# Softmax division moved from the attention weights to the attention output, query scale moved to the layout of the queries, and the SSD half of the output projection traced after attention

## Chip, cores and metric

One core of one Trainium2 chip. The metric is the device time of one execution of the whole kernel in microseconds (us), here the median of 3 runs.

## The reference, cut

Two layers, 512 tokens of 1024 features. Each layer has a mixer and a feed-forward part. The mixer projects its normalised input at once into the queries, keys and values of an attention group and into the inputs of a state-space (SSD) group; the two group outputs stand side by side and go through one output projection.

```python
q = rms_norm(q.reshape(b, l, N_Q_HEADS, HEAD_DIM), q_norm_w[i])   # 8 query heads of 64
k = rms_norm(k.reshape(b, l, N_KV_HEADS, HEAD_DIM), k_norm_w[i])  # 2 key heads
q = axial_rope(q, ...); k = axial_rope(k, ...)
# blocked_gqa, with q / sqrt(64):
s = jnp.einsum("bqgrd,bkgd->bgrqk", qi, k)
p = jax.nn.softmax(s, axis=-1)
attn_out = jnp.einsum("bgrqk,bkgd->bqgrd", p, v)
...
mixed = jnp.concatenate([attn_out, ssd_out], axis=-1)
x = x + jnp.einsum("ble,ed->bld", mixed, w_out[i])
```

## The kernel before, in words

All products run in pairs of reduced-precision operands: a weight or activation is split into a high part and a low part (`whi`/`wlo`, `xh`/`xl`), and `mm3` (lines 409 to 413) adds three matmuls for one product. The weights come in chunks through `Stream`: SP loads a chunk, ACT casts its high part (line 192), DVE or POOL subtracts the low part (line 193). `next` splits two chunks ahead.

The mixer of a layer is written as three generators that `drain` steps in turn: `att` (attention), `fill` (the projections of q, z and the convolution inputs, then the output projection) and `ssd`. The order in which they are stepped is the order of tracing. A scheduler at compile time then fixes the order on each engine: it plays the program on a model of the engines, and whenever an engine is free, it takes the instruction traced earliest among those that are ready; `tc.high_priority()` puts what is traced within it ahead of the rest. On the chip each engine runs its instructions in that fixed order.

Attention works on 8 blocks of a layer, each 128 queries (`c`, 4 of them) by 4 heads of one key head (`g`, 2 of them); the blocks of `g` = 0 come first. For a block, `queries` (line 650) copies the four heads into `qd`, each twice side by side (line 653, ACT), transposes them on PE (line 656) and splits them into `qh` (line 659, ACT) and `ql` (line 660, DVE). `attention` (line 663) then does for each of the 4 heads:

- two matmuls into the scores, 128 queries by 512 keys (lines 668 and 669, PE);
- the negated maximum of a row (line 671, DVE) and its product with the scale `qri` (line 672, DVE), the reciprocal norm of the query;
- the exponential with that scale and bias, and its row sum into `sm` (line 674, ACT);
- the reciprocal of the sum (line 675, DVE) and the division of the weights, 128x512, in place (line 679, DVE);
- four transposes (line 682, PE), their copy into `t_ring` (line 684, ACT, shown as L92), and for two heads together 16 small matmuls with the values (line 692, PE), whose result is copied into `qr` (line 694, ACT, shown as L92).

`qri` is worked out once for each `g` by a row of small DVE instructions (lines 637 and 285 to 291).

The SSD half of the output is the first half of `out_half` (line 787): 8 outputs of 12 matmuls each, added into `part` (line 795, DVE). It needs only the SSD group. It is traced once the SSD generator is done, while attention has some blocks left. After it and after attention, the attention output is cast and subtracted, four times (lines 854 and 855), and the attention half of `out_half` follows (line 933).

Of the kernel before, what the change touches and what calls it, by code (L numbers as in the profile page):

```python
# [15 lines left out]
F32 = mybir.dt.float32  # L16
# [3 lines left out]
ALU = mybir.AluOpType  # L20
# [16 lines left out]
NPAIR = (NF - PLAIN) // 2  # L37
SRAW = 6

NORM = "VVVV"  # L40
PTE = "AAAA"
GGE = "GG"
QDE, OUTE, _, YE, HE, WE, RAE, MLE, DSE = "AAVGVGVVG"
EB, GGB = 2, 4
DDW, DDE = 512, "A"
MORE = "VGGVG"
# [28 lines left out]
def bc(ap, shape, axis):  # L75
    return ap.unsqueeze(axis).broadcast_to(shape)
# [3 lines left out]
def tile_hybrid_encoder(ctx, tc, xt_d, par_d, rope_d, snw_d, w_kvdt, w_xbc, w_q, w_z, w_out, w_gate, w_up, w_down, out_d):  # L80
# [10 lines left out]
    def copy(e, out, in_):  # L91
        A.copy(out, in_) if e == "A" else (G if e == "G" else V).tensor_copy(out, in_)  # L92
# [353 lines left out]
    def mixer(l, norm, mx):  # L446
# [203 lines left out]
        def queries(c, g):  # L650

            qd = mx.tile([P, 4, 2, 64], F32, name="qd", tag="qd")
            copy(QDE, qd, bc(qr[:, c, 4 * g:4 * g + 4], [P, 4, 2, 64], 2))
            tp = bank("t")
            for j in range(4):
                T.transpose(tp[:, j * P:(j + 1) * P], qd[:, j].rearrange("p a d -> p (a d)"), ident)
            qh = mx.tile([P, S], F32R, name="qh", tag="qh", bufs=2)
            ql = mx.tile([P, S], F32R, name="ql", tag="ql", bufs=2)
            A.copy(qh, tp)
            V.tensor_tensor(ql, tp, qh.bitcast(F32), ALU.subtract)  # L660
            return qh, ql

        def attention(c, g, qh, ql):
            nm = mx.tile([P, 4], F32, name="nm", tag="nm", bufs=2)
            sm = mx.tile([P, 4], F32, name="sm", tag="sm", bufs=2)
            for j in range(4):
                s_ = bank("s")
                T.matmul(s_, lhsT=qh[:, j * P:(j + 1) * P], rhs=KK[:, g], start=True, stop=False)
                T.matmul(s_, lhsT=ql[:, j * P:(j + 1) * P], rhs=KK[:, g], start=False, stop=True)
                ri = qri[g][:, c, j:j + 1]  # L670
                V.tensor_reduce(nm[:, j:j + 1], s_, AX.X, ALU.max, negate=True)
                V.tensor_tensor(nm[:, j:j + 1], nm[:, j:j + 1], ri, ALU.mult)
                p_ = ring("p")
                A.activation(p_, s_, AF.Exp, bias=nm[:, j:j + 1], scale=ri, accum_out=sm[:, j:j + 1])
                V.reciprocal(sm[:, j:j + 1], sm[:, j:j + 1])
                if NORM[j] == "A":
                    A.activation(p_, p_, AF.Copy, scale=sm[:, j:j + 1])
                else:
                    (G if NORM[j] == "G" else V).tensor_scalar(p_, p_, sm[:, j:j + 1], None, ALU.mult)
                t_ = bank("t")  # L680
                for kt in range(NC):
                    T.transpose(t_[:, kt * P:(kt + 1) * P], p_[:, kt * P:(kt + 1) * P], ident)
                pt = merge(ring("t"), NC, P)
                copy(PTE[j], pt, merge(t_, NC, P))
                if j % 2 == 0:
                    first = pt
                    continue
                o_ = bank(O_BANK)

                for kt in range(NC):  # L690
                    for e, t2 in enumerate((first, pt)):
                        T.matmul(o_[64 * e:64 * e + 64, :P], lhsT=Vt[:, kt, g * 64:(g + 1) * 64],
                                 rhs=t2[:, kt], start=kt == 0, stop=kt == NC - 1)
                copy(OUTE, qr[:, c, 4 * g + j - 1:4 * g + j + 1].rearrange("p h d -> p (h d)"), o_[:, :P])
                yield
# [91 lines left out]
        def out_half(half, order, src, x, nxt=None):  # L787
            for n, m in enumerate(order):
                if n % 2 == 0:
                    wh, wl = W.next()  # L790
                ps = bank("a")
                for k in range(4):
                    o = (n % 2 * 4 + k) * P
                    mm3(ps, wh[:, o:o + P], wl[:, o:o + P], mixed, half * 4 + k, k == 0, k == 3)
                V.tensor_tensor(x[m], src[m], ps, ALU.add)
                if nxt is not None and m >= 4:
                    nxt.tile(m)
                    nxt.square(m)
                if m % 2:
                    yield  # L800
# [21 lines left out]
        def fill():  # L822
            for what in ORDER:
                i = int(what[1])
                if what[0] == "q":
                    yield from qproj(i)
                elif what[0] == "z":
                    yield from token_major(lambda c: bank("a"), op, 256, z_done(i))
                else:
                    xbc(i)  # L830
                    yield
                    if all(f"x{j}" in ORDER[:ORDER.index(what) + 1] for j in range(4, 8)):
                        done.append("BC")
                    if sum(w_[0] == "x" for w_ in ORDER[:ORDER.index(what) + 1]) == 8:
                        for c in range(3):
                            state(0, c)
                        for c in (3, 2, 1):
                            state(1, c)
                        done.append("conv")
            done.append("z")  # L840
            while "ssd" not in done:
                yield

            part = [mx.tile([P, S], F32, name=f"part{i}", tag=t) for i, t in enumerate(sorted(Htags))]
            part += [mx.tile([P, S], F32, name=f"part{6 + i}", tag="ee", bufs=EB) for i in range(2)]
            for k in range(KT):
                nc.sync.dma_start(part[k], (xt_d if l == 0 else x_save)[k])
            yield from out_half(1, range(KT), part, part)
            while "att" not in done:
                yield  # L850
            for j in range(4):
                src = qr.rearrange("p c (j a) d -> p j c (a d)", a=2)[:, j]
                h = mixed.h[j].rearrange("p (c q) -> p c q", c=NC)
                A.copy(h, src)
                tt(MLE, mixed.l[j].rearrange("p (c q) -> p c q", c=NC), src, h.bitcast(F32), ALU.subtract)
            Z["part"] = part

        def drain(*gens):
# [7 lines left out]
        def att():  # L866
            todo = [(c, g) for g in range(2) for c in range(NC)]
            ready = None
            for i, (c, g) in enumerate(todo):
                while g not in qri:  # L870
                    yield
                now = ready or queries(c, g)
                ready = None
                if i + 1 < len(todo) and todo[i + 1][1] in qri:
                    ready = queries(*todo[i + 1])
                yield from attention(c, g, *now)
            done.append("att")

        def finish(cs):
# [288 lines left out]
```

## Time and profile before

| | us |
|---|---|
| median of 3 runs | 1262.58 (1261.21 to 1265.16) |
| the profiled execution | 1260.2 |
| its span, first to last instruction | 1258.5 |
| mixer of layer 0, about | 0 to 282 |
| mixer of layer 1, about | 630 to 895 |

Engines: PE is TensorE's matmuls, PEld its weight loads, DVE VectorE, ACT ScalarE, POOL GpSimd, SP SyncE. The span is the part of the execution that the trace shows; 1.7 us of the profiled execution lie around it. Busy time of PE counts matmuls whose ends are modelled and overlap, so a PE that is busy throughout is not necessarily at its peak.

### The profile page before, as it was taken

How to read it: one execution, taken by the hardware profiler on the slowest of the kernel's cores; microseconds unless marked ns; L12 is line 12 of the kernel's file. 1: busy time of each engine (PE TensorE's matmuls, PEld its weight loads, DVE VectorE, ACT ScalarE, POOL GpSimd, SP SyncE). 2: the span in 40 equal slices, each digit the busy share in tenths (PEclk: the TensorE clock that was granted, in tenths of full speed). 3: DMA queues.
4: the chain of work that ended last, by engine and by line, in shares of the span. 5: the costliest groups of instructions: out<-in, count | busy, mean ns of one | idle time of the engine just before them, and what ended most of it. 6: DMA issues, size and time to landing. Idle time of an engine off the chain costs nothing.

```text
span 1258.5 us, 19786 instructions
## 1 busy us (share of the span) xinstructions
PE 1205.1 (96%) x7694; PEld 1066.4 (85%) x7694; DVE 962.1 (76%) x1593; ACT 620.1 (49%) x1147; POOL 249.3 (20%) x208
## 2 busy tenths in 40 slices
PE   6898998999999999999998999999999999999996
PEld 6787887687899899899897787777878999999995
DVE  8899789656887577577679989985688856856853
ACT  4566655634354244255455575753453533533544
POOL 6523655010200000000234255520120000000002
PEclk8999998999999999999999999989999999999998
DMA  5321122032434324321442202112243233243122
GB/s 170 104 72 51 34 68 77 17 101 65 154 96 143 89 83 132 88 87 32 135 135 89 67 30 72 55 40 72 94 144 88 98 117 113 74 120 114 34 63 80
DMA packets 47533, 110.04 MB, mean 87 GB/s; under 512 B 5424, under 2 KB 5936, under 8 KB 47440
## 3 DMA queue, kind: packets, MB, share of 16 engines
q1 hardware_dynamic: 47440, 108.79, 27.4%
q8 instruction: 60, 0.98, 0.3%
q14 instruction: 33, 0.27, 0.1%
HBM read 104.44 MB, written 4.33 MB: 86 GB/s over the span
## 4 chain that ended last, share of the span: by engine, by line
PE 76%; DVE 17%; ACT 3%; issue 2%; POOL 1%; DMA 1%; DVEq 0%; ACTq 0%; POOLq 0%
PE ps_a L1030 6%; PE ps_a L1029 5%; PE ps_a L1028 5%; PE ps_a L411 4%; PE ps_a L412 3%; PE ps_a L413 3%; PE ps_a L1075 3%; PE ps_a L1074 3%; PE ps_a L1076 3%; PE ps_s L1074 3%; PE ps_s L1075 3%; PE ps_s L1076 3%; PE ps_s L1030 3%; PE ps_s L1029 3%; PE ps_s L1028 3%; DVE u L594 3%
## 5 line engine op out<-in xcount | busy, mean ns | idle before, releaser
L192 ACT CAST whi<-wraw 128x512 fp32r<-128x512 f32 (+4 forms) x185 | 126.7, 713 | 231.7 <-PE ps_a L412 61.5
L192 ACT CAST whi<-sraw 128x1024 fp32r<-128x1024 f32 x126 | 131.7, 1050 | 141.3 <-DVE sraw L167 40.4
L193 DVE TENSOR_TENSOR wlo<-sraw,whi 128x1024 fp32r<-128x1024 f32 x126 | 153.6, 1223 | 46.5 <-ACT whi L192 46.3
L323 POOL TENSOR_TENSOR ssq<-ssq,sqt 128x512 f32<-128x512 f32 x17 | 25.7, 1511 | 679.5 <-ACT sqt L320 679.3
L193 DVE TENSOR_TENSOR wlo<-wraw,whi 128x512 fp32r<-128x512 f32 (+4 forms) x121 | 109.1, 911 | 49.8 <-ACT whi L192 48.8
L411 PE MATMUL ps_a<-xh,whi 128*128 128x512 f32 x320 | 126.3, 397 | 3.2 <-DVE a__9140 L971 1.6
L413 PE MATMUL ps_a<-xh,wlo 128*128 128x512 f32 x320 | 126.0, 394 | 0.0
L412 PE MATMUL ps_a<-xl,whi 128*128 128x512 f32 x320 | 125.7, 394 | 0.0
L193 POOL TENSOR_TENSOR wlo<-wraw,whi 128x512 fp32r<-128x512 f32 x64 | 91.1, 1441 | 97.8 <-ACT whi L192 90.7
L167 DVE TENSOR_TENSOR sraw<-sraw 128x1024 f32<-128x1024 f32 x72 | 88.0, 1222 | 1.0
L419 PE MATMUL ps_a<-whi,xh 128*128 128x256 f32 (+1 forms) x256 | 75.5, 297 | 7.9 <-ACT whi L192 7.8
L1030 PE MATMUL ps_a<-ss,wlo 128*128 128x256 f32 x288 | 81.7, 284 | 0.0
L1028 PE MATMUL ps_a<-ss,whi 128*128 128x256 f32 x288 | 81.5, 283 | 0.0
L1029 PE MATMUL ps_a<-ss,whi 128*128 128x256 f32 x288 | 81.5, 283 | 0.0
L1030 PE MATMUL ps_a<-s,wlo 128*128 128x256 f32 x288 | 81.1, 283 | 0.0
L1029 PE MATMUL ps_a<-s,whi 128*128 128x256 f32 x288 | 81.1, 283 | 0.0
L1028 PE MATMUL ps_a<-s,whi 128*128 128x256 f32 x288 | 79.8, 283 | 0.0
L420 PE MATMUL ps_a<-wlo,xh 128*128 128x256 f32 (+1 forms) x256 | 75.8, 296 | 1.7 <-DVE wlo L193 1.7
L411 PEld LDWEIGHTS ps_a<-xh,whi 128*128 128x128 f32 x320 | 60.2, 188 | 17.1 <-ACT s L989 4.0
L421 PE MATMUL ps_a<-whi,xl 128*128 128x256 f32 (+1 forms) x256 | 74.4, 293 | 0.0
L413 PEld LDWEIGHTS ps_a<-xh,wlo 128*128 128x128 f32 x320 | 60.4, 189 | 13.2 <-issue 0.8
L412 PEld LDWEIGHTS ps_a<-xl,whi 128*128 128x128 f32 x320 | 60.3, 188 | 12.4 <-DVE xl L809 0.4
(393 smaller groups left out, 3601.8 us busy)
## 6 DMA issues: line engine op xcount, KB each, us to landing
sraw<-in_w_gate SPq DMA_DIRECT2D x72, 256.0 KB, 3.8
sraw<-in_w_up SPq DMA_DIRECT2D x72, 256.0 KB, 3.8
wraw<-in_w_down SPq DMA_DIRECT2D x48, 384.0 KB, 3.1
wraw<-in_w_xbc SPq DMA_DIRECT2D x16, 512.0 KB, 3.3
wraw<-in_w_out SPq DMA_DIRECT2D x16, 512.0 KB, 3.3
wraw<-in_w_q SPq DMA_DIRECT2D x8, 512.0 KB, 3.2
wraw<-in_w_z SPq DMA_DIRECT2D x8, 512.0 KB, 3.6
wraw<-in_w_gate SPq DMA_DIRECT2D x8, 512.0 KB, 3.3
```

The costliest lines, as they stand in the source:

```text
L167: V.tensor_tensor(q[to], q[to], q[by], ALU.add)
L192: A.copy(hi[:, u], raw[:, u])
L193: (G if lo_pool else V).tensor_tensor(lo[:, u], raw[:, u], hi[:, u].bitcast(F32), ALU.subtract)
L411: T.matmul(ps, lhsT=wh, rhs=op.h[k], start=first, stop=False)
L412: T.matmul(ps, lhsT=wh, rhs=op.l[k], start=False, stop=False)
L413: T.matmul(ps, lhsT=wl, rhs=op.h[k], start=False, stop=last)
L420: T.matmul(ps, lhsT=xh, rhs=wl, start=False, stop=False)
L1028: T.matmul(out, lhsT=wh[:, o:o + P], rhs=x_[:, 0, i], start=first and i + j == 0, stop=False, skip_group_check=True)
L1029: T.matmul(out, lhsT=wh[:, o:o + P], rhs=x_[:, 1, i], start=False, stop=False, skip_group_check=True)
L1030: T.matmul(out, lhsT=wl[:, o:o + P], rhs=x_[:, 0, i], start=False, stop=i == 3, skip_group_check=True)
L1074: T.matmul(ps[:, cols], lhsT=w1[:, o:o + P], rhs=h, start=f == a, stop=False)
L1075: T.matmul(ps[:, cols], lhsT=w1[:, o:o + P], rhs=g, start=False, stop=False)
```

## The change

The weights stay undivided. The row sums of all 32 heads and query blocks of a layer are kept in one tile, `sums`, and the output is divided at the end by a new function, `normalize`: reciprocal of all sums, 4 transposes to bring heads onto partitions, a copy, then for each pair of heads one f32 matmul that spreads the 8x512 reciprocals over 128 partitions with a matrix of ones and zeros, a product with the output, and the same cast and subtraction as before. The scale `qri` is applied by the copy into `qd`, which becomes four copies of one head each; the product of line 672 goes. `att` ends with `normalize` under high priority, after the z projection, and the SSD half of the output is traced only after `att` has ended.

```diff
         def queries(c, g):
             qd = mx.tile([P, 4, 2, 64], F32, name="qd", tag="qd")
-            copy(QDE, qd, bc(qr[:, c, 4 * g:4 * g + 4], [P, 4, 2, 64], 2))
+            for j in range(4):
+                A.activation(qd[:, j], bc(qr[:, c, 4 * g + j], [P, 2, 64], 1), AF.Copy, scale=qri[g][:, c, j:j + 1])
...
+        sums = mx.tile([P, NC, 8], F32, name="sums")
+        def normalize():
+            sel = ring("p")[:8]
+            G.memset(sel, 0.0)
+            pick = merge(sel, 8, 64)
+            G.affine_select(out=pick, in_=pick, pattern=[[-1, 8], [0, 64]], compare_op=ALU.not_equal, fill=1.0,
+                            base=0, channel_multiplier=1)
+            rec = mx.tile([P, NC, 8], F32, name="rec")
+            V.reciprocal(rec, sums)
+            tp = bank("t")
+            for c in range(NC):
+                T.transpose(tp[:8, c * P:(c + 1) * P], rec[:, c], ident)
+            rows = ring("p")[:8]
+            A.copy(rows, tp[:8])
+            for j in range(4):
+                b = bank("s")
+                T.matmul(b, lhsT=sel[:, j * P:(j + 1) * P], rhs=rows, start=True, stop=True)
+                o = qr.rearrange("p c (j a) d -> p j c (a d)", a=2)[:, j]
+                V.tensor_tensor(o, o, merge(b, NC, P), ALU.mult)
+                h = merge(mixed.h[j], NC, P)
+                A.copy(h, o)
+                tt(MLE, merge(mixed.l[j], NC, P), o, h.bitcast(F32), ALU.subtract)
...
         def attention(c, g, qh, ql):
-                V.tensor_tensor(nm[:, j:j + 1], nm[:, j:j + 1], ri, ALU.mult)
                 p_ = ring("p")
-                A.activation(p_, s_, AF.Exp, bias=nm[:, j:j + 1], scale=ri, accum_out=sm[:, j:j + 1])
-                V.reciprocal(sm[:, j:j + 1], sm[:, j:j + 1])
-                if NORM[j] == "A":
-                    A.activation(p_, p_, AF.Copy, scale=sm[:, j:j + 1])
-                else:
-                    (G if NORM[j] == "G" else V).tensor_scalar(p_, p_, sm[:, j:j + 1], None, ALU.mult)
+                A.activation(p_, s_, AF.Exp, bias=nm[:, j:j + 1], accum_out=sums[:, c, 4 * g + j:4 * g + j + 1])
...
-            yield from out_half(1, range(KT), part, part)
             while "att" not in done:
                 yield
-            for j in range(4):
-                src = qr.rearrange("p c (j a) d -> p j c (a d)", a=2)[:, j]
-                h = mixed.h[j].rearrange("p (c q) -> p c q", c=NC)
-                A.copy(h, src)
-                tt(MLE, mixed.l[j].rearrange("p (c q) -> p c q", c=NC), src, h.bitcast(F32), ALU.subtract)
+            yield from out_half(1, range(KT), part, part)
...
                 yield from attention(c, g, *now)
+            while "z" not in done:
+                yield
+            with tc.high_priority():
+                normalize()
             done.append("att")
```

## Rows read from the trace of the kernel before

**Rows 1.** The page of the profile: its first part (busy time of each engine, share of the span, instructions) and the head of its fourth part (share of the span that each engine has of the chain of work that ended last).

```profile
PE 1205.1 (96%) x7694; PEld 1066.4 (85%) x7694; DVE 962.1 (76%) x1593; ACT 620.1 (49%) x1147; POOL 249.3 (20%) x208
...
PE 76%; DVE 17%; ACT 3%; issue 2%; POOL 1%; DMA 1%; DVEq 0%; ACTq 0%; POOLq 0%
```

**Rows 2.** Busy time of each engine by stretch. Columns: the stretch, its length, then for PE, PEld, DVE, ACT and POOL the busy us with the instruction count, the granted TensorE clock, the DMA share, GB/s. The first five are stretches of the two mixers in which attention runs, the last two those in which the SSD half of the output projection runs.

```profile
84.00:117.00 33.00, 29.24 (x175) 23.52 (x174) 32.09 (x58) 18.76 (x39) 14.02 (x10) 1.00 0.16 50
200.00:236.50 36.50, 30.28 (x208) 23.13 (x206) 32.13 (x85) 22.64 (x59) 13.67 (x12) 0.91 0.18 58
695.00:725.00 30.00, 29.40 (x166) 23.13 (x165) 28.90 (x57) 16.28 (x34) 9.31 (x7) 1.00 0.21 70
770.00:785.00 15.00, 14.09 (x95) 11.36 (x95) 14.19 (x28) 8.03 (x18) 11.71 (x11) 1.00 0.30 90
800.00:845.00 45.00, 40.12 (x286) 32.33 (x284) 42.66 (x106) 30.12 (x78) 19.54 (x18) 0.92 0.18 58
236.50:258.40 21.90, 21.90 (x106) 17.36 (x106) 10.38 (x17) 6.53 (x13) 0.00 (x0) 1.00 0.15 49
845.00:872.00 27.00, 27.00 (x145) 21.44 (x144) 12.43 (x23) 9.06 (x19) 0.00 (x0) 1.00 0.18 59
```

**Rows 3.** The chain of work that ended last, in order of time (start us, us, what): its pieces of half a microsecond or more on lines 672 and 679 and on the subtraction of line 855 (all subtractions of helper `tt` on DVE show as L95).

```profile
104.56 1.36 DVE p_ring L679
...
165.25 0.64 DVE nm L672
...
188.22 0.71 DVE nm L672
...
189.03 1.16 DVE p_ring L679
...
190.29 1.08 DVE p_ring L679
...
203.43 3.36 DVE xl L95 x2
206.79 1.13 DVE nm L672
...
700.67 1.84 DVE p_ring L679 x2
...
719.56 1.32 DVE p_ring L679
...
775.08 1.14 DVE nm L672
...
779.70 0.50 DVE p_ring L679
...
807.58 1.28 DVE p_ring L679 x2
...
813.08 1.69 DVE xl L95
...
815.92 0.60 DVE xl L95
```

**Rows 4.** Busy time by stretch of the instructions of one line alone, for the first five stretches of Rows 2; the sum over the five, in this order for line 672, line 675 and line 679.

```profile
sum 159.50, DVE 7.62; mean DVE 1.52
...
sum 159.50, DVE 5.03; mean DVE 1.01
...
sum 159.50, DVE 21.07; mean DVE 4.21
```

**Rows 5.** Who PE waited for (us in total, times, longest), 195 to 240 us and 800 to 845 us.

```profile
PE ps_m L775 <- DVE y L770: 4.2, 1, 4.2
...
PE ps_m L775 <- DVE y L770: 3.6, 1, 3.6
```

**Rows 6.** Busy time by stretch, columns as in Rows 2: the stretches right after those two waits.

```profile
209.00:217.00 8.00, 8.00 (x36) 6.15 (x35) 7.31 (x20) 0.27 (x1) 5.13 (x5) 0.57 0.29 99
...
815.00:830.00 15.00, 11.36 (x56) 9.54 (x58) 14.39 (x28) 3.88 (x9) 8.27 (x7) 0.77 0.44 141
```

**Rows 7.** The chain of work again, columns as in Rows 3: the product of a 128x128 f32 operand with 512 f32 columns of line 344, which runs as two instructions, and four transposes of a head.

```profile
40.06 0.86 PE ps_m L344 x2
...
139.28 0.44 PE ps_t L682 x4
```

**Rows 8.** Groups of instructions by line, each form apart: count, then busy us, mean ns, and idle time before with its releaser. The copy of four heads into `qd`, and the copy of 128 columns out of PSUM into `qr`.

```profile
L92 ACT COPY qd<-qr 128x512 f32<-128x512 f32 x16 | 10.1, 631 | 3.6 <-DVE qr L95 3.5
L92 ACT COPY qr<-ps_t 128x128 f32<-128x128 f32 x32 | 8.5, 267 | 13.9 <-PE ps_t L692 13.4
```

**Rows 9.** Instructions of one line (count: ns least/median/most, first and last start): the reciprocal of line 486, 64 columns.

```profile
L486 DVE RECIPROCAL sp<-sp x2: 545/550/554, 40.6 to 653.3; 128x64 f32<-128x64 f32 x2
```

**Rows 10.** Instructions in order of time (start us, us, engine, line, operation): the last cast and subtraction of lines 854 and 855 in layer 0, the first POOL instruction after the SSD group with the idle time before it; in layer 1 the last step of the scale `qri` for the second four heads, and the first copy into `qd` that belongs to them.

```profile
250.33 0.62 ACT L854 CAST xh<-qr 128x512 fp32r<-128x512 f32 x1
250.98 0.69 DVE L95 TENSOR_TENSOR xl<-qr,xh 128x512 fp32r<-128x512 f32 x1
...
268.62 1.86 POOL L323 TENSOR_TENSOR ssq<-ssq,sqt 128x512 f32<-128x512 f32 x1 [45.68 <-ACT sqt L320]
...
762.18 0.49 DVE L291 SCALAR_TENSOR_TENSOR qri<-qri1t,qri 128x16 f32<-128x16 f32 x1
...
777.26 0.62 ACT L92 COPY qd<-qr 128x512 f32<-128x512 f32 x1
```

More of the change, by code (lines that the diff above doesn't have):

```diff
@@ L38 @@
 SRAW = 6
-NORM = "VVVV"
 PTE = "AAAA"
 GGE = "GG"
-QDE, OUTE, _, YE, HE, WE, RAE, MLE, DSE = "AAVGVGVVG"
+OUTE, _, YE, HE, WE, RAE, MLE, DSE = "AVGVGVVG"
 EB, GGB = 2, 4
@@ L661, in queries @@
             return qh, ql
+        sums = mx.tile([P, NC, 8], F32, name="sums")
[20 more added lines that the diff above has]
+                tt(MLE, merge(mixed.l[j], NC, P), o, h.bitcast(F32), ALU.subtract)
         def attention(c, g, qh, ql):
             nm = mx.tile([P, 4], F32, name="nm", tag="nm", bufs=2)
-            sm = mx.tile([P, 4], F32, name="sm", tag="sm", bufs=2)
             for j in range(4):
@@ L669, in attention @@
                 T.matmul(s_, lhsT=ql[:, j * P:(j + 1) * P], rhs=KK[:, g], start=False, stop=True)
-                ri = qri[g][:, c, j:j + 1]
                 V.tensor_reduce(nm[:, j:j + 1], s_, AX.X, ALU.max, negate=True)
-                V.tensor_tensor(nm[:, j:j + 1], nm[:, j:j + 1], ri, ALU.mult)
                 p_ = ring("p")
-                A.activation(p_, s_, AF.Exp, bias=nm[:, j:j + 1], scale=ri, accum_out=sm[:, j:j + 1])
-                V.reciprocal(sm[:, j:j + 1], sm[:, j:j + 1])
-                if NORM[j] == "A":
-                    A.activation(p_, p_, AF.Copy, scale=sm[:, j:j + 1])
-                else:
-                    (G if NORM[j] == "G" else V).tensor_scalar(p_, p_, sm[:, j:j + 1], None, ALU.mult)
+                A.activation(p_, s_, AF.Exp, bias=nm[:, j:j + 1], accum_out=sums[:, c, 4 * g + j:4 * g + j + 1])
                 t_ = bank("t")
```

## The prediction

> **What bounds the kernel now.** Begin with the page: PE is busy 96% of the span and holds 76% of the chain of work that ended last, DVE 17% [rows 1]. Averages hide stages, so the second view is busy time by stretch. In the stretches of the mixers where attention runs, DVE is the full engine: 32.09 of 33.00 us, 28.90 of 30.00, 14.19 of 15.00, and in the two late ones 32.13 of 36.50 and 42.66 of 45.00 [rows 2], in which it also waits for others. Once the SSD half of the output runs, this turns round: PE is busy 21.90 of 21.90 and 27.00 of 27.00 us, DVE under half [rows 2]. So a mixer is a DVE stage followed by a PE stage, and what the change takes from DVE counts only in the first. The third view is the chain itself: it passes through the very instructions that go, in 14 pieces of half a microsecond or more [rows 3]. The fourth is what PE waits for: in either layer its longest wait near the end of attention, 4.2 and 3.6 us, is for an addition (line 770) that stands on DVE behind such instructions [rows 5], and after it the granted clock averages 0.57 and 0.77 [rows 6], between its two levels of 1.2 and 2.4 GHz.
>
> **The change part by part.**
>
> *A, DVE is relieved.* For each of 64 heads the scale product, the reciprocal and the division go. In the five DVE stretches they take 7.62 + 5.03 + 21.07 = 33.7 us [rows 4]; the early subtractions of line 855, for the heads of `g` = 0, move out of this crowd to the end and add 3.36 + 1.69 + 0.60 = 5.65 us [rows 3]. That is 39.4 us, the upper bound: it would all be gained if DVE alone set the pace. The pieces that the chain itself passes through are, layer 0, 1.36 + 0.64 + 0.71 + 1.16 + 1.08 + 3.36 + 1.13 = 9.4 us and, layer 1, 1.84 + 1.32 + 1.14 + 0.50 + 1.28 + 1.69 + 0.60 = 8.4 us [rows 3], 17.8 us together. This is the nearer figure, since a piece beside the chain needs another queue to move too; but in four of the five stretches DVE idles under 6% [rows 2], and there a removed instruction moves everything behind it up. I take a quarter of the way from the one to the other: 17.8 + 0.25 x 21.6 = 23.2 us. The lower bound is 10 us, about half the chain's pieces, if PE or the exponential is late next.
>
> *B, the clock.* A stretch of t us at a granted share s loses t(1 - s): 8.00 x 0.43 = 3.4 and 15.00 x 0.23 = 3.4 us [rows 6]. Both follow the waits for line 770 [rows 5]. In layer 0 the removed pieces just ahead of it (3.36 + 1.13) exceed the wait of 4.2; in layer 1 (1.69 + 0.60) they cover two thirds of 3.6. With shorter waits some of the loss should go; I take half, 3.4 us, of 0 to 6.9.
>
> *C, PE gets new work.* Nothing in the trace has 8 partitions and 512 f32 columns; the nearest is line 344, 0.86 us for 128 partitions and as many columns [rows 7]. Four of them are 3.44 us. Four transposes cost 0.44 [rows 7], here with 8 columns of weights each. That is 3.9 us a layer, 7.8 in all. They fall next to the SSD half, where PE has no idle time [rows 2], so I charge them in full; the other end is 0, if they run while PE still waits for the SSD group.
>
> *D, ACT.* One copy of 0.631 us becomes four, of 128 columns each; the nearest row is the 0.267 us copy out of PSUM [rows 8], so 4 x 0.267 - 0.631 = 0.44 us a block, 7.0 us for 16 blocks. The queries are laid out a block ahead, and ACT is busy 95.8 of the 159.5 us of the five stretches (18.76 + 22.64 + 16.28 + 8.03 + 30.12) [rows 2]. I charge 1 us of 0 to 7. The copy also has a new wait, for `qri`. On ACT the exponentials would queue behind it. But for the second group of layer 1 the scale is ready at 762.7 and the first copy starts at 777.26 [rows 10]: 14 us of cover, charged at nothing. Without it, the layout of a block (some 3 us) would show once for each group and layer.
>
> *E, the end of attention.* All sums must be there before the reciprocal. Then follow, one behind another: reciprocal of 32 columns, at most the 0.55 us of 64 [rows 9], transposes 0.44, a copy 0.62, the first spreading matmul 0.86 [rows 7], product 0.69, cast 0.62, subtraction 0.69 [rows 10], and for the other three pairs 2 x 0.69 each on DVE: 0.55 + 0.44 + 0.62 + 0.86 + 0.69 + 0.62 + 0.69 + 4.14 = 8.6 us. The cover is the SSD half: 21.9 us or more in which PE has other work and DVE is free for 11.5 [rows 2]. It was already what hid the end of attention, whose last cast came at 250.33, inside it [rows 10]. POOL's memset and selection have no later work to delay: POOL then idles until 268.62 [rows 10]. The products and casts need no queue but ACT's and DVE's; SP's loads of weights and of `part` are issued as before, though the split of the last SSD chunks is now traced behind attention. I charge E nothing while the SSD half fills it.
>
> *Sum.* -23.2 - 3.4 + 7.8 + 1.0 = -17.8 us on the profiled execution's 1260.2, so 1242.4. The median of the runs stands 2.4 above that execution; the same offset gives **1245 us**.
>
> **The rivals.**
>
> *PE's idle time is the cap.* In the five stretches PE is busy 29.24 + 30.28 + 29.40 + 14.09 + 40.12 = 143.1 of 159.5 us [rows 2]. If that busy time can't be pressed together, A and B are worth at most 16.4 us, and with C and D the time is 1262.6 - 16.4 + 8.8 = 1255. Against it: PE counts as busy for 8.00 of 8.00 us at a clock share of 0.57 [rows 6], so its busy time holds air. The Trainium skill (Perfetto Trace Analysis, Identifying the Most-Contended Engine) says that matmul busy share is no good measure of PE's headroom and that the share of weight loads should be read. By that rule the room is 159.5 less 113.5 us of PEld [rows 2], 46 us, and the cap would not bind, which leaves my sum as it is. Chance 0.20.
>
> *DVE was the whole bound.* The 39.4 us come in full, the clock stays up (6.9), and half of C falls into PE's idle time: 1262.6 - 39.4 - 6.9 + 3.9 + 1.0 = 1221. For it: DVE's busy share over 94% in four of the five stretches [rows 2]. Against it: the chain passes through less than half of that time [rows 3]. Chance 0.15.
>
> *PE waits out the normalisation.* PE runs in a fixed order. If the order made at compile time puts the spreading matmuls ahead of SSD products that are ready, PE stands through the chain of E less its own 1.3 us, 7.3 us a layer, and such a wait is followed by a low clock, as those of 4.2 and 3.6 us were [rows 5, 6], for 3.4 more, and B does not come. That is 2 x 10.7 = 21.4: 1262.6 - 23.2 + 21.4 + 8.8 = 1270, slower than before. It decides from (23.2 - 8.8) / 2 = 7.2 us of lost PE time a layer on. For it: high priority and tracing ahead of the SSD half invite it, and the model of the engines at compile time need not know the waits of the chip. Against it: the order picks among what is ready, and the SSD half is ready during that time in the trace before. Chance 0.15.
>
> **How the numbers follow.** Forecast 0.50, 1234 to 1256 (A some ten us larger or smaller); the cap 0.20; the whole bound 0.15; the wait 0.15. About 0.3%, 3.8 us, is what a measurement of this kernel can tell from no change, so "the same" is 1258.8 to 1266.4. Faster: 0.48 of the forecast, 0.14 of the cap (it reaches up with the upper ends of C and D), 0.15 of the whole bound: 0.77. Slower: 0.12 of the wait. The rest, 0.11, is the same. The range 1224 to 1266 leaves out half of the whole bound and most of the wait, about 0.19.
>
> **What the profile after would show.** A: lines 675 and 679 gone, DVE's busy time down by 30 us or more over the span, and the first output of the SSD half some 8 us or more earlier in each layer. B: no wait for line 770 over 2 us, and a granted share near 1 in the stretch behind it. C: 8 spreading matmuls near 0.86 us each. E: no wait of PE over 2 us between the last exponential and the attention half. The prediction is wrong if the SSD half starts no earlier, which makes PE or the exponential the bound, or if PE stands still for more than 7 us a layer around `normalize`.

## The result, and the profile after

The changed kernel takes 1269.22 us (median of 15 runs, 1265.40 to 1273.74) against 1261.30 of the kernel before (15 runs beside it): ratio 1.0055, 95% interval 1.0041 to 1.0069. It is slower by about 8 us, where 1245 was forecast and 1266 was the upper end. The profiled execution took 1272.4 us, 3.2 above the median, so its stretches show a little more loss than the runs.

The page of the changed kernel, the same lines as [rows 1]:

```profile
PE 1221.3 (96%) x7718; PEld 1074.8 (85%) x7718; DVE 921.7 (73%) x1411; ACT 625.9 (49%) x1197; POOL 249.8 (20%) x212
...
PE 76%; DVE 15%; ACT 3%; POOL 2%; issue 2%; DMA 1%; DVEq 0%; ACTq 0%; POOLq 0%
```

DVE was relieved as meant: 40.4 us less than in [rows 1]. But PE's busy time rose by 16.2 us, and DVE lost only two points of the chain. (Line numbers after: scaled copies 653, normalisation 665 to 687 with the spreading products on 682, the addition to `y` 788, its reader 793, finish's scaling of `xs` 912, the additions of the output halves 813.)

Two times in each layer tell where the time went (first addition of the SSD half to `part`, first addition of the attention half to `x`). In layer 0 the SSD half starts at 234.0 in place of 240.0 us, and the attention half at 271.1 in place of 263.9. In layer 1 it is 850.9 for 848.9, and 887.9 for 874.4; the same early DVE work of that layer (line 465 before, 464 after) comes at 638.0 in place of 632.4. So ahead of the SSD half there is a gain of 6.0 us in layer 0 and of some 3.6 in layer 1 (8 or more each were forecast), and behind it 13.3 and 11.4 us are lost. What PE does there, in order of time (start us, us, engine, line, what; the last products of the SSD half, the spreading products, the first of the attention half):

```profile
257.00 0.39 PE L411 MATMUL ps_a<-xl,whi 128*128 128x512 f32 x1
257.31 1.98 PE L682 MATMUL ps_s<-p_ring 8*128 8x512 f32 x4
...
260.35 1.43 PE L682 MATMUL ps_s<-p_ring 8*128 8x512 f32 x2
261.71 0.79 PE L410 MATMUL ps_a<-xh,whi 128*128 128x512 f32 x1
262.44 2.07 PE L682 MATMUL ps_s<-p_ring 8*128 8x512 f32 x2
264.44 0.80 PE L411 MATMUL ps_a<-xl,whi 128*128 128x512 f32 x1
265.03 0.63 PE L412 MATMUL ps_a<-xh,wlo 128*128 128x512 f32 x1
...
267.95 0.40 PE L412 MATMUL ps_a<-xh,wlo 128*128 128x512 f32 x1
268.18 0.40 PE L410 MATMUL ps_a<-xh,whi 128*128 128x512 f32 x1
```

The eight instructions of the four spreading products hold 1.98 + 1.43 + 2.07 = 5.48 us, with single output products wedged in between; before and after them such products follow each other 0.23 us apart, but at 264.44 to 265.03 the distance is 0.59. That is a lower clock. Busy time by slices of 2 us, columns as in [rows 2]:

```profile
258.00:260.00 2.00, 2.00 (x7) 0.89 (x6) 1.36 (x3) 0.62 (x1) 0.00 (x0) 1.00 0.00 0
260.00:262.00 2.00, 2.00 (x5) 0.58 (x3) 2.00 (x5) 1.66 (x3) 0.00 (x0) 0.76 0.05 12
262.00:264.00 2.00, 2.00 (x3) 0.50 (x2) 2.00 (x4) 0.62 (x1) 0.00 (x0) 0.50 0.00 0
264.00:266.00 2.00, 2.00 (x5) 1.27 (x5) 1.03 (x3) 0.62 (x1) 0.00 (x0) 0.50 0.81 262
266.00:268.00 2.00, 2.00 (x7) 1.58 (x6) 0.66 (x1) 0.00 (x0) 0.00 (x0) 0.54 0.01 4
268.00:270.00 2.00, 2.00 (x10) 1.64 (x9) 0.00 (x0) 0.00 (x0) 0.00 (x0) 1.00 0.00 0
```

PE counts as busy throughout and yet runs 3 to 7 products a slice in place of 10: the granted clock goes from 1.00 to 0.50, from 2.4 to 1.2 GHz, and is back at 268. The four slices from 260 lose 2 x (0.24 + 0.50 + 0.50 + 0.46) = 3.4 us. Layer 1 shows the same from 878 to 886 (0.71, 0.50, 0.50, 0.58).

Who PE waited for, the rows that answer to [rows 5], layer 0 and layer 1:

```profile
PE ps_m L793 <- DVE y L788: 4.3, 1, 4.3
...
PE ps_m L793 <- DVE y L788: 3.6, 1, 3.6
```

These two waits were to shrink, and are as long as they were, 4.3 and 3.6 us. What stood on DVE ahead of the addition to `y`, in order of time:

```profile
198.79 0.16 DVE L288 TENSOR_TENSOR yri0t<-yri 128x4 f32<-128x4 f32 x1
198.99 1.14 DVE L289 TENSOR_TENSOR yri0t<-yri0t,ym 128x4 f32<-128x4 f32 x1
200.16 1.20 DVE L290 SCALAR_TENSOR_TENSOR yri<-yri0t,yri 128x4 f32<-128x4 f32 x1
201.40 4.66 DVE L912 SCALAR_TENSOR_TENSOR xs<-xs,yri,snw 128x256 f32<-128x256 f32 x4
205.98 0.41 DVE L837 SCALAR_TENSOR_TENSOR gz<-zth,gz 128x256 f32<-128x256 f32 x1
206.31 0.68 DVE L788 TENSOR_TENSOR y<-y,ps_m 128x512 f32<-128x512 f32 x1
```

And on POOL at the same time:

```profile
198.84 5.14 POOL L192 TENSOR_TENSOR wlo<-wraw,whi 128x512 fp32r<-128x512 f32 x4 [3.44 <-ACT whi L191]
203.94 1.44 POOL L94 TENSOR_TENSOR gg<-gg,ee 128x512 f32<-128x512 f32 x1
```

While POOL subtracts, two operations on 128x4 elements take 1.14 and 1.20 us, where the one ahead of them, of the same size, took 0.16, and four scalings of 128x256 take 1.17 us each, where the median of that line is 0.48. The removed instructions are gone from this queue; others have moved up beside the same POOL work and are stretched in their place.

### The profile page after: what moved, and what is told of

It is laid out like the page before. It is cut to its first block, busy times and chain, and to the rows that moved or that the text cites. A ratio compares the mean times of both kernels' runs of the same rounds, so it can differ in the third digit from the quotient of the medians.

```text
span 1270.4 us, 19707 instructions
## 1 busy us (share of the span) xinstructions
PE 1221.3 (96%) x7718; PEld 1074.8 (85%) x7718; DVE 921.7 (73%) x1411; ACT 625.9 (49%) x1197; POOL 249.8 (20%) x212
## 4 chain that ended last, share of the span: by engine, by line
PE 76%; DVE 15%; ACT 3%; POOL 2%; issue 2%; DMA 1%; DVEq 0%; ACTq 0%; POOLq 0%
PE ps_a L1047 5%; PE ps_a L1046 5%; PE ps_a L1045 5%; PE ps_a L410 4%; PE ps_a L411 4%; PE ps_a L412 4%; PE ps_a L1091 3%; PE ps_a L1092 3%; PE ps_a L1093 3%; PE ps_s L1091 3%; PE ps_s L1092 3%; PE ps_s L1093 3%; PE ps_s L1047 3%; PE ps_s L1046 3%; PE ps_s L1045 3%; PE ps_t L710 2%
## 5 line engine op out<-in xcount | busy, mean ns | idle before, releaser
L411 PE MATMUL ps_a<-xl,whi 128*128 128x512 f32 x320 | 128.3, 402 | 0.0
```

The lines of the kernel that those rows point to most:

```text
L411: T.matmul(ps, lhsT=wh, rhs=op.l[k], start=False, stop=False)
```

## The experiments

Theory 1: the gain of A came in part, and the spreading products, with a low clock that I had not counted, cost more than it. Against it stood: DVE's relief brought nothing (PE's idle time was the cap), the bare chain of E costs, the new trace order costs. Medians are compared with the kernel before run beside each (1261.1 to 1263.7 us); brackets give the ratio to it with its 95% interval.

**No division at all.** All of `normalize` but the casts is left out:

```diff
-            sel = ring("p")[:8]
...
-                V.tensor_tensor(o, o, merge(b, NC, P), ALU.mult)
```

> This kernel leaves the division by the sums of the weights out altogether (no selection, reciprocal, transposes, spreading products, and no product with them; the early casts stay at the end, the queries stay scaled as laid out, the trace order stays changed), so its output is not divided. Theory 1, the spreading of the reciprocals on PE ate the gain: in the trace of the changed kernel the stretches from 257.31 to 267.95 and from 875.05 to 885.90 us hold 13 and 14 output products of 0.23 us, so 10.64 - 13 x 0.23 and 10.85 - 14 x 0.23, 7.6 us each, are lost to it. Expected 1269.2 - 15.3 = 1254 us, 0.6% below the kernel before. Theory 2, DVE's relief brought nothing because PE was the cap: the division hardly matters, the time stays at 1263 or above.

1250.87 us (0.9896, 0.9876 to 0.9916), where 1254 was expected. DVE's relief alone brings 11.9 us, and the division as written costs 18.3. Theory 1 holds, and Theory 2 falls. PE's two waits are still there, 4.7 and 3.3 us:

```profile
PE ps_m L777 <- DVE y L772: 4.7, 1, 4.7
...
PE ps_m L777 <- DVE y L772: 3.3, 1, 3.3
```

**Spreading over 128 rows, 120 of them zero.**

```diff
-            sel = ring("p")[:8]
+            sel = ring("p")
...
-            rows = ring("p")[:8]
-            A.copy(rows, tp[:8])
+            rows = ring("p")
+            G.memset(rows, 0.0)
+            A.copy(rows[:8], tp[:8])
```

> The spreading products contract over 128 rows, 120 of them zero, in place of 8; columns and count stay, and one more memset of 128x512 goes to POOL. Theory 1a, the granted clock of 0.50 around them comes with eight rows in use: it stays near 1, and the 3.4 us a layer that the shares 0.76, 0.50, 0.50, 0.54 of four 2-us slices cost come back, 1269.2 - 6.8 = 1262 us. Theory 1b, it comes with these products whatever the rows (f32 columns, waits between them): the same clock, 1269 us.

1262.09 us (0.9992, 0.9980 to 1.0005), 7.1 less than the changed kernel. Instructions of the spreading line (count: ns least/median/most), first in the changed kernel, then here:

```profile
L682 PE MATMUL ps_s<-p_ring x16: 587/692/1217, 257.3 to 879.8; 8*128 8x512 f32 x16
```

```profile
L683 PE MATMUL ps_s<-p_ring x16: 590/592/697, 255.0 to 868.8; 128*128 128x512 f32 x16
```

And the slices in which the products lie here (254.96 to 259.7 us):

```profile
256.00:258.00 2.00, 2.00 (x7) 1.14 (x7) 1.81 (x3) 1.05 (x2) 0.00 (x0) 1.00 0.00 0
258.00:260.00 2.00, 2.00 (x7) 1.13 (x6) 2.00 (x5) 1.23 (x3) 0.00 (x0) 1.00 0.06 12
260.00:262.00 2.00, 2.00 (x9) 1.42 (x8) 2.00 (x4) 0.77 (x2) 0.00 (x0) 1.00 0.24 39
```

The clock stays at 1.00, in layer 1 too (864 to 874 us). At full clock the recorded length of an instruction is the same (587 and 590 ns at least). Two products among output products still take a little more room with eight rows: from the start of the output product ahead of them to that of the second one behind, 2.56 us (257.00 to 259.56 in the changed kernel) against 2.17 here (254.73 to 256.90). That 0.4 us, for two or three such groups in each layer, is the smaller part of the 7.1; the larger is the clock. Theory 1a holds: 6.8 us were expected.

**The chain taken away, eight rows kept.** One column of each spread bank is copied aside, and the casts take the undivided output:

```diff
-                V.tensor_tensor(o, o, merge(b, NC, P), ALU.mult)
+                V.tensor_copy(rec[:, 0, j:j + 1], b[:, :1])
```

> The changed kernel with all of the division's work except its last step: reciprocals are transposed and spread by the 8-row products, of each of which one column is copied aside, but the output of attention is not multiplied by them, so the casts wait for none of it and the output is not divided. If the 18 us between the changed kernel and the one without division are PE's own time for these products and the low clock that goes with them: 1266 to 1269 us. If a good part is the chain at the end (the attention half of the output waits for products and casts): 1258 to 1262 us.

1263.07 us (1.0002, 0.9988 to 1.0016), between the two expectations. Its spreading products and the slices that hold them (257.70 and 263.47 us, two pairs with output products between):

```profile
L682 PE MATMUL ps_s<-p_ring x16: 587/587/692, 257.7 to 875.8; 8*128 8x512 f32 x16
```

```profile
256.00:260.00 4.00, 4.00 (x14) 2.13 (x13) 1.00 (x3) 0.00 (x0) 0.00 (x0) 1.00 0.03 7
260.00:264.00 4.00, 4.00 (x17) 2.88 (x16) 2.31 (x4) 1.14 (x2) 0.00 (x0) 1.00 0.09 17
264.00:268.00 4.00, 4.00 (x15) 2.55 (x14) 1.24 (x4) 1.24 (x2) 0.00 (x0) 1.00 0.30 116
```

Here eight rows did not lower the clock, and the chain's removal is worth 6.2 us, about what the low clock cost. With the chain but without the low clock it was 1262.1, so the chain's own waits cost about nothing. In these traces the clock fell only where both came together, products of eight rows and the chain that lets little else run between them. It did so in both layers of the changed kernel and of the two runs below that keep its spreading (here one slice of each, first with the SSD half's subtractions on DVE, then with all of them), and in no layer of this run and the one before:

```profile
254.00:256.00 2.00, 2.00 (x4) 0.79 (x3) 1.78 (x3) 0.62 (x1) 0.00 (x0) 0.50 0.00 0
```

```profile
244.00:246.00 2.00, 2.00 (x4) 0.78 (x3) 1.17 (x3) 0.18 (x1) 0.00 (x0) 0.50 0.59 184
```

Why it falls there, no run tells.

**Spreading by transposes.** ACT copies each reciprocal over 64 columns, and PE transposes 128x128 blocks:

```diff
+                wide = ring("p").rearrange("p (c a d) -> p c a d", c=NC, a=2)
+                A.copy(wide, bc(rec[:, :, 2 * j:2 * j + 2], [P, NC, 2, 64], 3))
+                for c in range(NC):
+                    T.transpose(b[:, c * P:(c + 1) * P], wide[:, c].rearrange("p a d -> p (a d)"), ident)
-                T.matmul(b, lhsT=sel[:, j * P:(j + 1) * P], rhs=rows, start=True, stop=True)
```

> The reciprocals are spread in another way: ACT copies each over 64 columns, and 16 transposes of 128x128 a layer bring them to the output's layout, in place of four 8-row products of 512 columns and their transposes. Theory 1: 16 x 0.11 = 1.8 us a layer at full clock replace 7.6, so 1269.2 - 11.6 = 1258 us. Theory 3, what costs is the chain at the end of attention (PE or the attention half waits for products and casts, whatever spreads the sums): the time stays within 3 us of 1269.

1254.09 us (0.9928, 0.9909 to 0.9947), below the 1258 expected: the same division for some 3 us (3.2 by the medians) in place of 18.3, faster than both kernels. Theory 3 falls.

**The trace order.** In the kernel before, and then in the run with transposes, the SSD half is put on the other side of the wait for attention:

```diff
-            yield from out_half(1, range(KT), part, part)
             while "att" not in done:
                 yield
...
+            yield from out_half(1, range(KT), part, part)
```

> The kernel before, with the SSD half of the output traced behind the end of attention and its casts, as the change does; the rest stays. Theory 1: PE's order is made from what is ready, so this alone changes nothing, 1259 to 1264 us. Theory 4, the new trace order puts the attention tail among the SSD half's products and holds up the attention half: most of the loss is here, 1266 us or more.

> As the run that spreads the reciprocals by transposes (1254 us), but with the SSD half of the output traced ahead of the wait for attention, as in the kernel before. If the trace order is worth nothing, as in the kernel before: 1252 to 1256 us. If the division needs it, because its transposes and products then stand behind 96 products of the SSD half: the attention half starts some 4 to 6 us later in each layer, 1262 to 1266 us.

1263.07 us (1.0000, 0.9985 to 1.0015) and 1256.84 (0.9952, 0.9934 to 0.9971). In the kernel before the order is worth nothing. With the division the old order is 2.7 us behind 1254.09 by the medians; the intervals of the two overlap, so this stays open.

**The scale put back** into maximum and exponential, in the run without division:

```diff
+                V.tensor_tensor(nm[:, j:j + 1], nm[:, j:j + 1], ri, ALU.mult)
...
-                A.activation(p_, s_, AF.Exp, bias=nm[:, j:j + 1], accum_out=sums[:, c, 4 * g + j:4 * g + j + 1])
+                A.activation(p_, s_, AF.Exp, bias=nm[:, j:j + 1], scale=ri, accum_out=sums[:, c, 4 * g + j:4 * g + j + 1])
```

> As the run without any division (1251 us; the output is not divided here either), but the queries are laid out unscaled by one copy, and the scale is again a product on the maximum (64 of 128x1 on DVE) and the scale of the exponential. Theory 7, what DVE is given back counts at half its size, as my term A took it: 64 products held 7.6 us of DVE and stood in the chain, 1254 to 1256 us. Theory 8, only the divisions themselves counted, and ACT's four copies in place of one cost what the products saved: 1249 to 1252 us.

1251.20 us (0.9908, 0.9887 to 0.9928), against 1250.87. The scaling of the queries as laid out is worth nothing on balance, within some 3 us: Theory 8.

**POOL's subtractions moved to DVE.** The size of A was still open. In the run with transposes the low parts of the SSD half's weights are made on DVE:

```diff
-            stream(w_out[l, 1, i], 1024, 1, 512)
+            stream(w_out[l, 1, i], 1024, 0, 512)
```

> As the run that spreads the reciprocals by transposes (1254 us), and the subtractions that split the weights of the SSD half (L192, 8 of 128x512 a layer, 1.28 us each on POOL) go to DVE. PE's wait for the addition to y is still 4.3 and 3.6 us there, with four scalings of xs on DVE ahead of it that take 4.66 us in layer 0 while POOL subtracts beside them, and 1.67 in layer 1. Theory 5, DVE's instructions are stretched by what POOL does beside them: the four in layer 0 take 1.9 us, the waits fall below 2 us, with part of the low clock behind them, and 16 subtractions of about 0.65 us on DVE cost little: 1246 to 1251 us. Theory 6, DVE's stretch has nothing to do with POOL: the four stay at 4.66 us, and DVE gets 10 us more work, 1254 to 1260 us.

1244.34 us (0.9863, 0.9839 to 0.9888): 9.8 less, with 16 instructions more on DVE. DVE ahead of the addition to `y`, in order of time, and PE's waits for it in the two layers:

```profile
196.56 2.69 DVE L904 SCALAR_TENSOR_TENSOR xs<-xs,yri,snw 128x256 f32<-128x256 f32 x4
199.17 0.68 DVE L192 TENSOR_TENSOR wlo<-wraw,whi 128x512 fp32r<-128x512 f32 x1
199.77 0.68 DVE L780 TENSOR_TENSOR y<-y,ps_m 128x512 f32<-128x512 f32 x1
```

```profile
PE ps_m L785 <- DVE y L780: 1.4, 1, 1.4
...
PE ps_m L785 <- DVE y L780: 1.4, 1, 1.4
```

The four scalings take 2.69 us in place of 4.66, the waits 1.4 and 1.4 in place of 4.3 and 3.6. Theory 5 holds, though it expected 1.9 us for the four and 1246 or more in all; POOL still makes one product of 1.46 us beside them, from 197.11. The same edit was then made in other kernels, and more of POOL's subtractions were moved (first z0 and z1, then all 32 of a layer):

```diff
-POOL_LO = "x3 x5 x7 z0 z1 x4 x6 q1 x1".split()
+POOL_LO = "x3 x5 x7 x4 x6 q1 x1".split()
```

```diff
-POOL_LO = "x3 x5 x7 z0 z1 x4 x6 q1 x1".split()
+POOL_LO = "".split()
```

> The kernel before, with the weights of the SSD half split on DVE in place of POOL (8 subtractions of 128x512 a layer). Theory 9: there DVE is the full engine ahead of the SSD half, so 16 subtractions of 0.69 us (11 us) take back what the shorter wait for y gives (4.2 and 3.6 us and the low clock behind it): 1258 to 1266 us. Theory 10: POOL's stretch costs the kernel before as much as the changed one: 1249 to 1253 us.

> The run without any division (1251 us; the output is not divided here), with the same 8 subtractions a layer on DVE. Both theories expect about 10 us less, 1241 us, as between the two runs that spread the reciprocals by transposes. What tells them apart is the distance to the kernel before with the same edit, that is, what DVE's relief brings where POOL no longer stretches the work ahead of the addition to y: theory 9, the missing half of my term A was held back by that wait, 18 us or more; theory 10, it was never there, 9 to 13 us.

> The changed kernel with its 8-row spreading products, and the same 8 subtractions a layer on DVE. If the spreading costs what it costs whatever goes on ahead of the SSD half: 18 us above the run without division with the same edit, so about 1259 us. If part of that 18 us was the wait for y and its low clock: nearer, 1250 to 1254 us.

> As the fastest run that divides (1244 us: reciprocals spread by transposes, weights of the SSD half split on DVE), and the weights of z0 and z1 split on DVE too, 8 more subtractions of 128x512 a layer. If POOL's work still stretches DVE there: 1238 to 1242 us. If DVE has become short again: 1246 us or more.

> The kernel before, with the weights of the SSD half, of z0 and of z1 split on DVE (16 subtractions a layer in place of POOL's). Where DVE still divides every weight it is full ahead of the SSD half: 1252 to 1260 us, so that DVE's relief by the change is worth 16 us or more beside it. If POOL's stretch is all that matters: 1246 us, 7 less than with the SSD half's weights alone.

> As the fastest run (1237 us: reciprocals spread by transposes, weights of the SSD half, z0 and z1 split on DVE), and all other weights of the mixers that POOL splits on DVE too, 16 more subtractions a layer (22 us in all). If POOL's work beside DVE still holds it up: 1230 to 1235 us. If DVE is then the full engine again, as in the kernel before: 1240 to 1250 us.

> The kernel before, with every weight of the mixers split on DVE in place of POOL (32 subtractions of 128x512 a layer, 44 us on DVE in all). If POOL's subtractions beside DVE are what held the crowded stretches up, whatever DVE has to do: 1232 to 1238 us, some 14 below 1246. If DVE, which still divides all weights here, has no room for them: 1244 us or more, and the change is what makes the room, worth 22 us or more.

> The changed kernel with its 8-row spreading products, and every weight of the mixers split on DVE. If the spreading still costs 12 to 16 us more than the transposes that spread (1222 us with the same edit): 1234 to 1238 us. If PE has room for it by now: below 1230.

Median us, with the ratio to the kernel before:

| subtractions moved to DVE | kernel before | changed kernel | no division | transposes |
|---|---|---|---|---|
| none | 1261.30 | 1269.22 (1.0055) | 1250.87 (0.9896) | 1254.09 (0.9928) |
| SSD half | 1253.09 (0.9922) | 1256.50 (0.9955) | 1236.54 (0.9788) | 1244.34 (0.9863) |
| and z0, z1 | 1245.90 (0.9870) | | | 1237.16 (0.9802) |
| all | 1236.87 (0.9791) | 1234.09 (0.9777) | | 1221.86 (0.9684) |

The interval of each is about 0.002 to either side (0.9661 to 0.9708 for the last). In the kernel before, the SSD half's subtractions alone bring 9.7 us beside its own runs of before (1262.74), though DVE is its full engine: Theory 10 there. The run without division fell by 14.3 us, where both theories expected 10. The distance between the two, 1253.09 - 1236.54 = 16.6 us, lies between what the theories named. It is 4.7 more than the 11.9 without the edit, about what the intervals of these runs leave open together: that the wait had held back a part of A is likely, not shown. The changed kernel with the same edit, 1256.50, is 20.0 us above the run without division (its low clock is there too), so the cost of the spreading did not shrink. With z0 and z1 the two columns fall by 7.2 us each, and with all to 1236.87 (1232 to 1238 expected) and 1221.86, the second 8 us below what was expected at best: POOL's stretch, not DVE's own work, held these stretches up, in the kernel before as in the others. The changed kernel then falls to 1234.09, as expected of a spreading that still costs 12.2 us against the transposes, and is 2.8 us below the kernel before with the same edit, with overlapping intervals. With the transposes the change is worth 15.0 us there (1236.87 - 1221.86). The fastest is 1221.86 us, 3.2% below the kernel before. Page lines and one group of DVE instructions from 84 to 200 us (count, then busy us, mean ns, idle before), first with transposes and POOL as it was:

```profile
PE 1200.1 (96%) x7726; PEld 1064.4 (85%) x7726; DVE 921.2 (74%) x1411; ACT 628.8 (50%) x1203; POOL 249.3 (20%) x208
```

```profile
L767 DVE SCALAR_TENSOR_TENSOR gg<-st,dt,gg 128x128 f32<-128x128 f32 x32 | 19.2, 658 | 2.4 <-POOL gg L94 2.4
```

and with all subtractions on DVE:

```profile
PE 1188.8 (97%) x7726; PEld 1058.9 (87%) x7726; DVE 911.2 (75%) x1475; ACT 629.1 (52%) x1203; POOL 167.2 (14%) x144
```

```profile
L767 DVE SCALAR_TENSOR_TENSOR gg<-st,dt,gg 128x128 f32<-128x128 f32 x32 | 11.6, 420 | 0.0
```

DVE has 64 subtractions more, of 0.69 us at the median, 44 us in all, and is busy 10 us less. The same 32 products on `gg` take 420 ns each in place of 658. So some 54 us of DVE's busy time had been stretch, an estimate that takes all else on DVE as unchanged.

**The pairs of `g` = 0 divided early**, as soon as their four blocks are done, without and with the SSD half's subtractions on DVE:

```diff
                 yield from attention(c, g, *now)
+                if i == 3:
+                    normalize(0)
```

> As the run that spreads the reciprocals by transposes (1254 us), but the two pairs of heads of g = 0 are divided as soon as their four blocks are done, and only those of g = 1 at the end of attention. If the end of attention is covered there (2.0 us between the last output of the SSD half and the first of the attention half, as without any division): no change, 1252 to 1256. If half of its chain still shows: 1250 or less. If DVE's work ahead of the SSD half counts in full: two products and two subtractions of 0.69 us in each layer, 1257.

> Both edits that helped together: reciprocals spread by transposes with the pairs of g = 0 divided early (1251 us), and the 8 subtractions a layer on DVE (10 us less beside the same kernel without the early pairs). If they add up: 1241 us. If dividing early had only shortened the wait for y (1.7 us in place of 3.6 in layer 1), which is gone by now: 1244 us as without it.

1251.13 us (0.9912, 0.9891 to 0.9933) and 1243.86 (0.9853, 0.9831 to 0.9876). The first is 3.0 below 1254.09, with overlapping intervals, and PE's longest wait for `y` there is 1.7 us; the second equals 1244.34. With that wait gone, dividing early brings nothing: the end of attention is covered.

## Why the prediction was wrong, step by step

- **A, the first step that failed.** -23.2 was forecast. The run without division gives -11.9, with D and the query scale in it; put back, the scale changed nothing, so this is the divisions'. I had read pieces of the chain at their length in the trace, 3.36 us for two subtractions and 1.13 for a product on 128x1 [rows 3], as DVE's own time. A subtraction of that form takes 0.69 us in the same trace [rows 10], and these are the divisions and the products on 128x1 (count: ns least/median/most):

```profile
L679 DVE TENSOR_SCALAR p_ring<-p_ring,sm x64: 470/486/1522, 86.6 to 848.0; 128x512 f32<-128x512 f32 x64
L672 DVE TENSOR_TENSOR nm<-nm,qri x64: 140/150/1222, 84.2 to 846.2; 128x1 f32<-128x1 f32 x64
```

  At 0.49, 0.15 and 0.69 us the 14 pieces come to some 7.7 us in place of 17.8 (an estimate); the 11.9 measured lie between. The rest was stretch beside POOL, which passes on to whatever runs there next. The 32 products on `gg` of layer 0, before and after the change:

```profile
L757 DVE SCALAR_TENSOR_TENSOR gg<-st,dt,gg 128x128 f32<-128x128 f32 x32 | 14.0, 495 | 0.0
```

```profile
L775 DVE SCALAR_TENSOR_TENSOR gg<-st,dt,gg 128x128 f32<-128x128 f32 x32 | 19.2, 656 | 2.4 <-POOL gg L94 2.4
```

  Without POOL's subtractions for the SSD half, A is 16.6 us by the medians. No run brought the 39.4 of "the whole bound".
- **B, failed.** Forecast -3.4 from shorter waits. Both waits kept their length, behind other instructions. In that stretch (columns as in [rows 2]) the kernel before and the run without division have the clock at 0.89, and with the SSD half's subtractions on DVE that run has it at 1.00, with 4.4 us more of PE busy:

```profile
200.00:230.00 30.00, 23.84 (x153) 18.59 (x152) 26.49 (x65) 17.76 (x47) 13.67 (x12) 0.89 0.21 71
```

```profile
200.00:230.00 30.00, 24.04 (x166) 19.12 (x162) 22.23 (x43) 17.83 (x48) 13.35 (x12) 0.89 0.22 71
```

```profile
200.00:230.00 30.00, 28.47 (x196) 21.59 (x195) 19.17 (x43) 18.15 (x50) 7.61 (x8) 1.00 0.21 67
```

- **C, mis-sized.** Forecast 7.8, measured 11 to 12 without the low clock (1262.1 and 1263.1 against 1250.9). A product takes 0.99 us (1.98 for two) and not the 0.86 of line 344 [rows 7]: 8 x 0.99 = 7.9 us, with the 0.6 us of four transposes in each layer 9.1. Some 2 to 3 us more were not traced to a row.
- **D, not measured by itself.** 1.0 of 0 to 7 was charged. The four copies hold 5.0 us more of ACT than the one (625.5 us busy without division, 620.5 with the scale put back). Together with the products that they replace (7.6 us of DVE, stretch included) they came out at nothing, so neither has a size of its own.
- **E, the second step that failed.** "I charge E nothing while the SSD half fills it": PE indeed waited for nothing long there (0.3 us for the first addition of the attention half). But I asked only whether PE would stand still. It was busy with products of eight rows, its clock fell to 0.50, and the last of them and the output products behind ran at about half speed for some 6 us a layer. That is 7 us in all, for which there was no term. It was in none of the signs either: the SSD half did start earlier and PE did not stand still around `normalize`, so neither of the two signs of being wrong appeared.
- **The rivals.** "PE waits out the normalisation" gave 1270, near the result, and named the place and a low clock, even its 3.4 us a layer. The nearness is luck, for its mechanism was not what happened: the 7.3 us a layer of standing still never came, A was half of what it assumed, and the clock fell with PE busy, not after a wait. "PE's idle time is the cap" put 16.4 us as the most that A and B could bring. A came to 16.6 without the SSD half's subtractions on POOL, but with all of POOL's subtractions gone as well the kernel lost 40 us, and PE's busy time fell from 1205.1 [rows 1] to 1188.8 with 32 instructions more: it was no cap. With this the rule of the Trainium skill (Perfetto Trace Analysis, Identifying the Most-Contended Engine), that matmul busy share does not measure PE's headroom, agrees.
- **The sum.** Forecast -23.2 - 3.4 + 7.8 + 1.0 = -17.8; measured -11.9 + 0 + 11 + 7 + 0 = +6, against +7.9 in the runs. The kernel before took 1262.8 us beside the run without division and 1261.3 beside the changed kernel; these 1.5 us are the difference.

## What to carry to other kernels

Before a removed instruction is priced at its length in the trace, compare it with the shortest of its form: what is longer may belong to whatever ran beside it, and can stay in the kernel when the instruction goes, as it did here. A wait shrinks only if nothing else moves up into the queue ahead of it. Work given to PE has two prices, its time and what its shape does to the clock of the work behind it: here spreading with full 128x128 blocks was 15 us cheaper than with eight rows, and the granted clock right behind showed half of it.

## What was not expected of the hardware

- Eight-row products close together took PE from 1.00 to 0.50 of its clock while it counted as busy almost without a gap; the same products over 128 rows left it at 1.00, and so did eight-row products with output products between.
- POOL's work lengthens DVE's: an operation on 128x4 took 1.14 to 1.20 us beside POOL's subtractions in place of 0.16. Moving 64 subtractions from POOL, 1.33 us each at the median, to DVE, 0.69 each, lowered DVE's busy time by 10 us and the kernel with transposes by 32.2. The Trainium skill (Perfetto Trace Analysis, Optimizing Scalar/DVE Operations) says that the two share an SBUF read port, so that work moved from one to the other may not help. These durations agree with it: here it paid to take the work back from POOL.
